# Two-layer trunk on Trainium2: forty residual tiles of the gate weights made on GpSimd instead of VectorE

## Chip, cores and metric

The kernel runs on one core of a Trainium2 chip. The metric is the device time of one execution in microseconds (us); the time of a kernel is the median of its runs. A core has TensorE (PE, matrix products; its weight loads are shown apart as PEld), VectorE (DVE), ScalarE (ACT), GpSimd (POOL) and SyncE (SP, which here issues DMAs). Each engine works through its own queue in order and waits on semaphores for the others.

## The reference

For 256 tokens of width 2048, two layers in float32:

```python
for l in range(DEPTH):
    h = rms_norm(x, pre_mix_norm[l])
    m = hybrid_mixer(h, l, ...)          # in-projection, two kinds of attention, o-projection
    x = x + rms_norm(m, post_mix_norm[l])
    h = rms_norm(x, pre_ffn_norm[l])
    f = (silu(h @ w_gate[l]) * (h @ w_up[l])) @ w_down[l]      # 2048 -> 5632 -> 2048
    x = x + rms_norm(f, post_ffn_norm[l])
```

The case is about `h @ w_gate` and `h @ w_up`.

## The kernel before, in words

**Every weight is used once, in two pieces.** The weights come from memory as tiles of 128 x 2 x 512 float32 (512 KB): one *K pair*, that is 2 x 128 rows of the inner dimension, by 512 columns. They are stored in the order of use (`weights_in_turn`). For each tile SP issues a DMA (L230 into a `raw` buffer of 4, or L219 into a `G` buffer of 3), ACT makes `hi`, the tile rounded to the PE's short float32 format (`float32r`, L351), and VectorE makes the residual `lo = raw - hi` (L354). `hi` and `lo` have six buffers each. The tokens are split the same way into `sh` and `sl`, and a product is three matmuls: sh·hi + sh·lo + sl·hi (`product`, L1116 to L1118).

**Gate and up.** The 5632 columns are cut into 11 chunks of 512. A chunk runs over 8 K pairs (`kp`, in the order 0 to 7; chunk 0 has an order of its own), each with a gate tile and an up tile. It has four sums in PSUM banks, `c11`, `c12`, `c21`, `c22`: two halves of the tokens, each with gate and up. Most K pairs go through `eight`: eight products of 128x128 by 512. Some, in each chunk `SEVEN = (2, 4, 5, 6)`, in chunk 0 (4, 6), in chunk 1 (4, 5, 6), in chunks 7 and 9 (2 to 6), go through `seven`, a scheme of Strassen's kind with seven products. It needs sums of the weights: GpSimd's queue issues an accumulating DMA that adds a part of the gate tile onto the up tile `T` as it loads (L298), VectorE makes two further sums in place, t2 (L334) and G (L335, which overwrites the gate tile), and the sums are split like the weights (ACT L319, VectorE L320, tiles `Th`, `Tl`). The gate tile of such a pair lies in a `G` buffer, and its own `hi` and `lo` must be made before L335 overwrites it. The seven products put four extra sums (p1, p6, p7, q5) into the other four PSUM banks.

**The end of a chunk.** After the last `seven` of a chunk ACT and VectorE fold the four extra sums into four SBUF tiles `w` (`shared_part`, ACT copy L1157, VectorE L1158 to L1161). With that their banks come free, and the next chunk's `c` sums start in them. When the last K pair is done, VectorE adds the `c` banks to `w` (L1308, L1310), ACT makes the silu (L1309), and VectorE multiplies (L1311, two SBUF inputs). A little later PE transposes the result (L1317) and ACT copies it to `act`, the input of the down projection.

**What sets the order.** The program is written in program order, `weights()` makes the tiles four ahead of their use (`LOOKAHEAD`), and a scheduler orders each engine's queue when the program is built. Two hints around the change: `behind()` has the first two `lo` made after a `shared_part` come behind its last sum in VectorE's queue, and `after_rests()` has some other VectorE work come behind the latest `lo`, for which each VectorE `lo` is appended to the list `rests`.

So around a chunk's end VectorE's queue holds, mixed: the last splits of the old chunk, the first splits of the new one (kp 0, 1, 2), the four sums of `shared_part`, and the sums of the `c` banks.

Of the kernel before, what the change touches and what calls it, by code (L numbers as in the profile page):

```python
# [9 lines left out]
F32 = mybir.dt.float32  # L10
# [3 lines left out]
ALU = mybir.AluOpType  # L14
# [10 lines left out]
FF = 5632  # L25
CW = 512
# [22 lines left out]
FORESEEN = {7: (3, 5), 9: (3, 5)}  # L49
AHEAD_AT = 8  # L50
AHEAD_PACE = 2
FORM_AT = {(0, 1): 4, (0, 2): 6, (0, 5): 5, (1, 3): 2, (4, 3): 3}
DOWN_SEVEN = ((4, 7, 10, 12, 15, 17, 20), (3, 5, 8, 10, 13, 15, 18))

# [22 lines left out]
def weight_order():  # L77

    order = []

    def queue_pair(name, l, kp, c):
        order.append((name, l, kp, c))
        return len(order) - 1

    plan = []
    sevens, plain, own = set(), set(), set()
    for l in range(L):
        lay = {"in": {}, "o": {}, "gate": {}, "up": {}, "down": {}}
        for n, (ca, cb) in enumerate(PAIRS):
            for kp in IN_ORDER if n else range(KT // 2):  # L90
                lay["in"][ca, kp] = queue_pair("w_in", l, kp, ca)
                lay["in"][cb, kp] = queue_pair("w_in", l, kp, cb)
                if kp in IN_NOW[n]:
                    plain.add(lay["in"][cb, kp])
        order_o = [(c, kp) for kp in KP_O for c in (0, 1)]
        order_o += [(c, kp) for kp in LATE_O for c in (2, 3)] + [(c, kp) for c in (2, 3) for kp in LAST_O]
        lay["order_o"] = order_o
        for c, kp in order_o:
            lay["o"][c, kp] = queue_pair("w_o", l, kp, c)
            if c == 3 and kp in O_SEVEN:  # L100
                own.add(lay["o"][c, kp])
        for c in range(FF // CW):
            for kp in FIRST_ORDER if c == 0 else range(KT // 2):
                lay["gate"][c, kp] = queue_pair("w_gate", l, kp, c)
                lay["up"][c, kp] = queue_pair("w_up", l, kp, c)
                if kp in gate_sevens(c):
                    sevens.add(lay["up"][c, kp])
        for half in range(2):
            for kp in range(FF // P // 2):
                for c in (2 * half, 2 * half + 1):  # L110
                    lay["down"][c, kp] = queue_pair("w_down", l, kp, c)
                if kp in DOWN_SEVEN[half]:
                    sevens.add(lay["down"][2 * half + 1, kp])
        plan.append(lay)
    return order, plan, sevens, plain, own
# [48 lines left out]
def kernel(  # L164
# [15 lines left out]
    nc = tc.nc  # L180
# [19 lines left out]
    order, plan, sevens, plain, own = weight_order()  # L200
    stream = [weights_in_turn[i].rearrange("p (k n) -> p k n", k=2) for i in range(len(order))]

    ready = {}
    raws, loads = [], []
    fed = [0]

    def fetch(upto):
        while len(raws) < min(upto, len(stream)):
            i = len(raws)
            for j in range(i, min(i + EARLY + 1, mix_raw[3])):  # L210
                if j in sevens and j not in sums and not (j in foreseen and j > i + 1):
                    summed(j)
            if i in sevens:
                raws.append(sums[i])
                continue
            if i + 1 in sevens:
                g = mix_raw[0].tile([P, 2, CW], F32, tag="G", bufs=mix_raw[1], name=f"G{i}")
                with not_ahead(i):
                    loads.append(nc.sync.dma_start(g, stream[i]))  # L219
                raws.append(g)  # L220
                continue
            if i in own or i + 1 in own:
                raw = mix_pool[0].tile([P, 2, CW], F32, tag="v", bufs=2, name=f"V{i}")
            elif i in plain or i + 1 in plain:
                raw = late_room([P, 2, CW], f"GU{i}")
            else:
                raw = wpool.tile([P, 2, CW], F32, tag="raw", bufs=4, name=f"raw{i}")
            mixing = bool({i, i + 1} & (own | plain))
            with not_ahead(i) if mixing else nullcontext():
                loads.append(nc.sync.dma_start(raw, stream[i]))  # L230
            raws.append(raw)
            if not mixing:
                usual.append((i, loads[-1]))
# [10 lines left out]
    def foresee(l):  # L244
# [4 lines left out]
        def summed_up(i):  # L249
            g, u = tiles[i]  # L250
            k = kept.tile([P, 4, CW], F32, name=f"foreseen{i}")
            with after_rests():
                sums_in_place(g, u, True)
            nc.gpsimd.dma_start(k[:, 0:2, :], u)
            nc.gpsimd.dma_start(k[:, 2:4, :], g)
            foreseen[i] = k

        for n, i in enumerate(jobs):
            tiles[i] = [x_pool[0].tile([P, 2, CW], F32, tag="W", bufs=2 * len(jobs), name=f"{q}{i}") for q in ("Gf", "Tf")]
            for t, j in zip(tiles[i], (i - 1, i)):  # L260
                with in_turn():
                    nc.sync.dma_start(t, stream[j])
                yield AHEAD_PACE
            if n:
                summed_up(jobs[n - 1])
            yield AHEAD_PACE
        yield AHEAD_PACE
        summed_up(jobs[-1])
# [72 lines left out]
    def feed(upto):  # L341
        fetch(upto)
        while fed[0] < min(upto, len(stream)):
            i = fed[0]
            raw = raws[i]
            if i in sevens or i in plain or i in own:
                ready[i] = mixed_weights(i)
                fed[0] += 1
                continue
            hi = wpool.tile([P, 2, CW], F32R, tag="hi", bufs=6, name=f"hi{i}")  # L350
            nc.scalar.activation(hi, raw, AF.Copy)  # L351
            lo = wpool.tile([P, 2, CW], F32R, tag="lo", bufs=6, name=f"lo{i}")
            with behind():
                rest = nc.vector.tensor_tensor(out=lo, in0=raw, in1=hi.bitcast(F32), op=ALU.subtract)  # L354
            ready[i] = (hi, lo)
            fed[0] += 1
            rests.append(rest)
# [4 lines left out]
    def behind():  # L362

        if held[1] == 0:
            return nullcontext()
        held[1] -= 1
        return tc.issue_after(held[0].ins)

    def after_rests():

        return tc.issue_after(rests[-1].ins)
# [5 lines left out]
    def weights(i, ahead):  # L377
        feed(i + 1 + ahead)
        return ready[i]
# [20 lines left out]
    def put_away(nm, n):  # L400

        if n == 0:
            away.append(kept.tile([P, NT, D], F32, name=f"away_{nm}"))
        t, h = divmod(n, 2)
        with in_turn():
            nc.sync.dma_start(away[-1][:, t, h * D // 2 : (h + 1) * D // 2], xs[t][h])
# [760 lines left out]
    for l in range(L):  # L1167
# [17 lines left out]
        for n, (c, kp) in enumerate(plan[l]["order_o"][:16]):  # L1185
# [5 lines left out]
            if n in (9, 11):  # L1191
                kp = O_SEVEN[(n - 9) // 2]
# [4 lines left out]
        for kp in LATE_O:  # L1197
            i, j = (plan[l]["o"][c, kp] for c in (2, 3))
# [6 lines left out]
            hi, lo = weights(i, LOOKAHEAD)  # L1205
# [13 lines left out]
        with tc.manual_schedule(engines={mybir.EngineType.Activation, mybir.EngineType.DVE}):  # L1219
            feed(idx + 6)  # L1220
            for n, (c, kp) in enumerate(last_o):
                unit({0: accs[c, 0]}, mix, idx + n, kp, (0,), False, kp == LAST_O[-1], 0)
                if kp == LAST_O[-1]:
                    evac_sum(pool, accs[c, 0], mg, ssm, gpost, c, 0, f"o{l}")
            rescale(mg, ssm, 0, f"o{l}")
            for n, (c, kp) in enumerate(last_o):
                feed(idx + 7 + n)
                fetch(min(idx + 12 + n, idx + 12))
                unit({1: accs[c, 1]}, mix, idx + n, kp, (1,), False, kp == LAST_O[-1], 0)
                transposed(0, 32 + l * KT, xT, cols=(n,))  # L1230
                if (c, kp) == (2, LAST_O[-1]):
                    evac_sum(pool, accs[2, 1], mg, ssm, gpost, 2, 1, f"o{l}", True)
# [17 lines left out]
        def pair_sums(kp):  # L1250
            f = pool.tile([P, 2, S], F32, tag="t2", name=f"f{l}_{kp}")
            for kk in range(2):
                st = xT[2 * kp + kk]
                nc.vector.tensor_tensor(out=f[:, kk, :], in0=st[:, 0, :].bitcast(F32), in1=st[:, 1, :].bitcast(F32), op=ALU.add)
            forms[kp] = token_sums(pool, gu if kp in SEVEN else None, len(SEVEN), f[:, 0, 0:P], f[:, 1, 0:P], f[:, 0, P:S], f[:, 1, P:S], f"{l}_{kp}")
# [18 lines left out]
        for c in range(FF // CW):  # L1274
# [9 lines left out]
            for n, kp in enumerate(order):  # L1284
                if n == 1 and c in AWAY_AT:
                    put_away(f"ffn{l}", AWAY_AT.index(c))
                if (c, n) in FORM_AT:
                    with after_rests():
                        pair_sums(FORM_AT[c, n])
                if kp not in mine:  # L1290
# [41 lines left out]
        for half in range(2):  # L1332
# [74 lines left out]
            for t in range(NT):  # L1407
# [4 lines left out]
                for c in cc:  # L1412
                    for kp in range(nkp - tail, nkp):
# [3 lines left out]
                        hi, lo = weights(plan[l]["down"][c, kp], LOOKAHEAD)  # L1417
# [66 lines left out]
```

## Time and profile before

| | us |
|---|---|
| median of 3 runs | 2190.61 (2189.62 to 2191.96) |
| the profiled execution: its span | 2189.2 |
| PE busy | 2174.7 (99%) |
| VectorE busy | 1921.7 (88%) |
| ACT busy | 1378.0 (63%) |
| GpSimd busy | 144.2 (7%) |
| SP's DMA queue, share of 16 engines' span | 58.9% |

The profile is of one further execution; it lists a span, from the first to the last instruction, and no other time of its own, so the span is what sums are made against. It stands 1.4 us under the median of the runs. The engines' busy times don't add up to the span, since they work beside each other. In a timeline a row is: start, duration, engine, line, operation, out<-in, shape, how many rows of the same kind were taken together, and in brackets the idle time before it and what ended it. Instructions of one engine overlap a little: the next one of VectorE starts about 0.08 us before the last one ends, so a 1.22 us instruction takes 1.14 us of the queue; a PE matmul of 0.39 us takes 0.23.

### The profile page before, as it was taken

The page shows a single profiled execution, that of the slowest core. Times are in us where ns is not written, and L with a number is a line of the kernel's source. Part 1 is how long each engine was busy: PE and PEld are TensorE (multiplying, and loading weights), DVE is VectorE, ACT ScalarE, POOL GpSimd, SP SyncE. Part 2 cuts the span into 40 slices and gives each one's busy share as a digit, 9 for nine tenths or more (in the row PEclk, how much of TensorE's full clock was granted, in tenths as well). Part 3 has the DMA queues.
Part 4 walks back from the last instruction along what each step waited for, and adds up shares of the span by engine and source line. Part 5 has one row for each costly group of instructions (what it writes and reads, how often), then busy time and mean ns, then how long its engine had stood idle before and what let it go on. Part 6 is the DMA issues. An engine that isn't in the chain of part 4 may idle for free.

```text
span 2189.2 us, 28686 instructions
## 1 busy us (share of the span) xinstructions
PE 2174.7 (99%) x9980; PEld 1787.4 (82%) x9980; DVE 1921.7 (88%) x2647; ACT 1378.0 (63%) x2063; POOL 144.2 (7%) x199
## 2 busy tenths in 40 slices
PE   9999999999999999999999999999999999999998
PEld 7888888788888888888878888887788888888886
DVE  7888659999999999989878886699999999999997
ACT  7666665756656666666665656657566566666664
POOL 1100000010010000000010000000000100000000
PEclk9999999999999999999999999999999999999999
DMA  9545577587687786767465555775866877867673
GB/s 322 194 164 173 192 243 267 184 274 234 206 282 235 229 273 210 245 210 257 146 240 173 183 173 183 256 258 195 269 214 226 274 241 232 263 213 234 207 264 101
DMA packets 146033, 489.30 MB, mean 224 GB/s; under 512 B 16592, under 2 KB 17616, under 8 KB 145376
## 3 DMA queue, kind: packets, MB, share of 16 engines
q1 hardware_dynamic: 127712, 450.72, 58.9%
q0 software_dynamic: 17600, 36.22, 8.3%
q8 instruction: 78, 1.28, 0.2%
q10 hardware_dynamic: 576, 0.54, 0.1%
q14 instruction: 67, 0.55, 0.1%
HBM read 470.63 MB, written 16.78 MB: 223 GB/s over the span
## 4 chain that ended last, share of the span: by engine, by line
PE 92%; DVE 5%; ACT 1%; issue 1%; DMA 1%; DVEq 0%; ACTq 0%
PE c L1117 9%; PE c L1118 9%; PE c L1116 9%; PE in L1116 7%; PE in L1118 7%; PE in L1117 7%; PE dn L1368 4%; PE dn L1366 4%; PE dn L1365 4%; PE p L1117 2%; PE p L1118 2%; PE p L1116 2%; PE o L601 2%; PE o L603 2%; PE o L602 2%; DVE lo L354 1%
## 5 line engine op out<-in xcount | busy, mean ns | idle before, releaser
L354 DVE TENSOR_TENSOR lo<-raw,hi 128x1024 fp32r<-128x1024 f32 x514 | 615.2, 1219 | 90.7 <-ACT hi L351 89.8
L351 ACT ACTIVATE hi<-raw 128x1024 fp32r<-128x1024 f32 x514 | 531.3, 1055 | 183.1 <-DMA raw<-in_weights_in_turn_dram 51.3
L1116 PE MATMUL c<-hi,xF 128*128 128x512 f32 x806 | 317.2, 394 | 0.1
L1117 PE MATMUL c<-lo,xF 128*128 128x512 f32 x806 | 314.4, 390 | 1.2 <-DVE lo L354 1.0
L1118 PE MATMUL c<-hi,xF 128*128 128x512 f32 x806 | 314.0, 390 | 0.0
L1117 PEld LDWEIGHTS c<-lo,xF 128*128 128x128 f32 x806 | 151.5, 188 | 33.2 <-DVE lo L354 3.3
L1118 PEld LDWEIGHTS c<-hi,xF 128*128 128x128 f32 x806 | 151.3, 188 | 32.0 <-DVE xF L525 0.4
L1116 PEld LDWEIGHTS c<-hi,xF 128*128 128x128 f32 x806 | 151.4, 188 | 30.3 <-ACT xF L520 0.5
L298 POOL DMA_DIRECT2D T<-in_weights_in_turn_dram x106 | 92.2, 869 | 1257.8 <-DMA T<-in_weights_in_turn_dram 434.6
L1365 PE MATMUL dn<-hi,jh 128*128 128x512 f32 x432 | 168.2, 389 | 0.0
L1366 PE MATMUL dn<-lo,jh 128*128 128x512 f32 x432 | 168.1, 389 | 0.0
L354 DVE TENSOR_TENSOR lo<-G,hi 128x1024 fp32r<-128x1024 f32 x114 | 138.8, 1218 | 21.1 <-ACT hi L351 21.0
L319 ACT ACTIVATE hi<-T 128x1024 fp32r<-128x1024 f32 x114 | 119.7, 1050 | 41.9 <-PE c L1118 23.9
L320 DVE TENSOR_TENSOR lo<-T,hi 128x1024 fp32r<-128x1024 f32 x114 | 138.8, 1217 | 3.2 <-ACT hi L319 2.3
L351 ACT ACTIVATE hi<-G 128x1024 fp32r<-128x1024 f32 x114 | 120.0, 1053 | 30.1 <-PE c L1118 17.4
L319 ACT ACTIVATE Th<-G 128x1024 fp32r<-128x1024 f32 x106 | 111.8, 1055 | 36.8 <-DVE G L335 35.3
L320 DVE TENSOR_TENSOR Tl<-G,Th 128x1024 fp32r<-128x1024 f32 x106 | 129.1, 1218 | 5.5 <-ACT Th L319 5.3
L1368 PE MATMUL dn<-hi,jl 128*128 128x512 f32 x432 | 133.0, 390 | 0.0
L1116 PE MATMUL in<-hi,xT 128*128 128x512 f32 x328 | 131.0, 401 | 1.1 <-ACT hi L921 1.1
L1116 PE MATMUL in<-hi,xI 128*128 128x512 f32 x328 | 131.2, 401 | 0.0
L335 DVE TENSOR_TENSOR G<-G,T 128x1024 f32<-128x1024 f32 x106 | 129.3, 1220 | 1.7
L1117 PE MATMUL in<-lo,xI 128*128 128x512 f32 x328 | 128.1, 390 | 0.3 <-DVE lo L354 0.3
(485 smaller groups left out, 4786.7 us busy)
## 6 DMA issues: line engine op xcount, KB each, us to landing
raw<-in_weights_in_turn_dram SPq DMA_DIRECT2D x514, 512.0 KB, 4.7
G<-in_weights_in_turn_dram SPq DMA_DIRECT2D x114, 512.0 KB, 5.8
T<-in_weights_in_turn_dram SPq DMA_DIRECT2D x106, 512.0 KB, 6.4
T<-in_weights_in_turn_dram POOLq DMA_DIRECT2D x106, 256.0 KB, 7.2
GU<-in_weights_in_turn_dram SPq DMA_DIRECT2D x32, 512.0 KB, 6.5
Gf<-in_weights_in_turn_dram SPq DMA_DIRECT2D x8, 512.0 KB, 6.0
Tf<-in_weights_in_turn_dram SPq DMA_DIRECT2D x8, 512.0 KB, 6.7
V<-in_weights_in_turn_dram SPq DMA_DIRECT2D x8, 512.0 KB, 5.2
```

The source lines that it names most:

```text
L298: nc.gpsimd.dma_start(sums[i][:, 0, :], stream[i - 1][:, 0, :], accum_op=ALU.add)
L319: nc.scalar.activation(h, w, AF.Copy)
L320: nc.vector.tensor_tensor(out=l, in0=w, in1=h.bitcast(F32), op=ALU.subtract)
L335: nc.vector.tensor_tensor(out=g, in0=g, in1=t2.unsqueeze(1).to_broadcast([P, 2, CW]), op=ALU.add)
L351: nc.scalar.activation(hi, raw, AF.Copy)
L354: rest = nc.vector.tensor_tensor(out=lo, in0=raw, in1=hi.bitcast(F32), op=ALU.subtract)
L1116: nc.tensor.matmul(a, sh, hi, start=first, stop=False, skip_group_check=open_sums[0])
L1117: nc.tensor.matmul(a, sh, lo, start=False, stop=False, skip_group_check=open_sums[0])
L1118: nc.tensor.matmul(a, sl, hi, start=False, stop=last, skip_group_check=open_sums[0])
L1365: nc.tensor.matmul(accs[c, t], sh, hi[:, kk, :], start=first, stop=False, skip_group_check=open_sums[0])
L1366: nc.tensor.matmul(accs[c, t], sh, lo[:, kk, :], start=False, stop=False, skip_group_check=open_sums[0])
L1368: nc.tensor.matmul(accs[c, t], sl, hi[:, kk, :], start=False, stop=last, skip_group_check=open_sums[0])
```

## The change

For the gate tiles of the second and third K pair (kp 1 and 2) in chunks 1 to 10 of both layers, 2 x 10 x 2 = 40 tiles, GpSimd computes `lo = raw - hi`, the same subtraction, in place of VectorE. All other residuals stay on VectorE. Of the 40 tiles 22 are plain (`raw`: kp 1 everywhere, and kp 2 in chunk 1) and 18 are gate tiles of a `seven` (`G`: kp 2 in chunks 2 to 10). A helped tile isn't appended to `rests`, and `behind()` doesn't count it. The buffers and DMAs are the same.

```diff
@@ -49,6 +49,7 @@
+HELPED = (1, 2)
...
@@ -200,6 +201,8 @@
+    helped = {lay["gate"][c, kp] for lay in plan for c in range(1, FF // CW) for kp in HELPED}
+
...
@@ -350,6 +353,11 @@
             hi = wpool.tile([P, 2, CW], F32R, tag="hi", bufs=6, name=f"hi{i}")
             nc.scalar.activation(hi, raw, AF.Copy)
             lo = wpool.tile([P, 2, CW], F32R, tag="lo", bufs=6, name=f"lo{i}")
+            if i in helped:
+                nc.gpsimd.tensor_tensor(out=lo, in0=raw, in1=hi.bitcast(F32), op=ALU.subtract)
+                ready[i] = (hi, lo)
+                fed[0] += 1
+                continue
             with behind():
                 rest = nc.vector.tensor_tensor(out=lo, in0=raw, in1=hi.bitcast(F32), op=ALU.subtract)
             ready[i] = (hi, lo)
```

## The prediction, as it was put on record

> **What bounds the kernel now.** First the head of the page, then gate/up cut into windows (columns: window, its length, busy time and count of PE, PEld, DVE, ACT and POOL, clock, DMA share, GB/s). In layer 0 chunk 1 runs from about 441 to 484.3 us and chunks 2 to 10 from there to 858.1; the third window is layer 1's chunk 1.
>
> ```profile
> span 2189.2 us, 28686 instructions
> ...
> PE 2174.7 (99%) x9980; PEld 1787.4 (82%) x9980; DVE 1921.7 (88%) x2647; ACT 1378.0 (63%) x2063; POOL 144.2 (7%) x199
> ```
> ```profile
> 441.00:484.30 43.30, 42.66 (x190) 34.47 (x189) 41.41 (x56) 25.03 (x29) 4.37 (x5) 1.00 0.80 257
> 484.30:858.10 373.80, 373.67 (x1683) 308.98 (x1682) 352.71 (x386) 233.11 (x270) 27.82 (x32) 1.00 0.73 236
> 1530.00:1573.00 43.00, 41.98 (x186) 33.57 (x185) 40.41 (x54) 24.52 (x29) 3.82 (x5) 1.00 0.79 253
> ```
>
> PE is the bound. Over nine chunks it stands still for 373.80 - 373.67 = 0.13 us, so nothing done for VectorE can win anything there. Only the two chunks 1 hold something: 0.64 and 1.02 us. VectorE is nearly full beside it: 352.71 of 373.80, 39.2 a chunk of 41.5. Its waits in chunks 3 to 10 (us in total, times, longest) say where it has room:
>
> ```profile
> DVE lo L354 <- ACT hi L351: 9.5, 6, 1.8
> DVE w L1158 <- PE p L1118: 6.4, 7, 1.6
> ```
>
> It waits for inputs that ACT and PE have not made, so in these chunks it is ahead of need.
>
> **The price of one piece on GpSimd.** Forty tiles (kp 1 and 2, ten chunks, two layers) leave VectorE; the built program has 2557 VectorE instructions for 2597 and 244 for 204 on GpSimd, all else counted alike. No 128x1024 subtraction on GpSimd is in this trace. Its small ones are, with VectorE rows of the same moments:
>
> ```profile
> 48.60 0.46 POOL L874 TENSOR_TENSOR ra<-tok,rope_sb 128x128 f32<-128x128 f32 x1 [12.19 <-DMA lams<-in_lambda_k_dram]
> 49.02 0.32 POOL L875 TENSOR_TENSOR rb<-tok,rope_sb 128x64 f32<-128x64 f32 x1
> ...
> 52.91 1.54 POOL L874 TENSOR_TENSOR ra<-tok,rope_sb 128x128 f32<-128x128 f32 x1
> ...
> 96.04 0.33 POOL L875 TENSOR_TENSOR rb<-tok,rope_sb 128x64 f32<-128x64 f32 x1
> ```
> ```profile
> 52.90 1.23 DVE L354 TENSOR_TENSOR lo<-GU,hi 128x1024 fp32r<-128x1024 f32 x1 [1.50 <-ACT hi L351]
> 54.04 0.95 DVE L324 TENSOR_TENSOR GU<-GU,GU 128x512 f32<-128x512 f32 x1
> ...
> 95.98 1.37 DVE L1000 TENSOR_TENSOR w<-in,w 128x512 f32<-128x512 f32 x2 [0.46 <-PE in L1118]
> ```
>
> Sixty-four elements more cost 0.14 us: 2.2 ns an element, 0.18 + 1024 x 2.2 = 2.4 us for a tile. That is an estimate over a factor of eight; 2.1 to 2.55 covers a row's rounding. VectorE takes 1.14 a tile, start to start. **The two exclude each other.** GpSimd's 0.46 job begun at 52.91 lasted 1.54: it ended at 54.45, 0.32 after VectorE's two-operand subtraction ended at 54.13. The next one of VectorE's, 128x512, then took 0.95, against 0.68 for that shape below. So beside VectorE's SBUF-SBUF work a GpSimd piece starts when VectorE's instruction ends and then holds VectorE off for about 2.28 us (2.4 less what overlaps). Sums that read PSUM are spared: two of them at 95.98 took 1.37, or 0.69 each, with a GpSimd piece running. A tile moved therefore costs VectorE between -1.14 (all beside PSUM sums or idle time) and 2.28 - 1.14 = +1.14.
>
> The Trainium skill, page "SBUF — State Buffer", section "SBUF: two separate sides", says the same of a lock between a GpSimd operation and a VectorE one with two SBUF inputs, and page "Perfetto Trace Analysis", section "Optimizing Scalar/DVE Operations", warns that offloading between these two might not help because of it. By that rule alone the change is the second rival below; the rows agree on the lock, and show that it spares PSUM sums.
>
> **Chunks 3 to 10.** One chunk's end, 6 to 7, by timelines of ACT, VectorE and PE; the last VectorE row is mid-chunk, 20 us earlier:
>
> ```profile
> 685.53 1.06 ACT L351 ACTIVATE hi<-raw 128x1024 fp32r<-128x1024 f32 x1
> ...
> 693.86 1.05 ACT L351 ACTIVATE hi<-G 128x1024 fp32r<-128x1024 f32 x1
> ```
> ```profile
> 684.60 1.22 DVE L320 TENSOR_TENSOR Tl<-G,Th 128x1024 fp32r<-128x1024 f32 x1
> ...
> 687.59 0.69 DVE L1158 TENSOR_TENSOR w<-p,w 128x512 f32<-128x512 f32 x1 [0.64 <-PE p L1118]
> ...
> 689.65 0.68 DVE L1161 TENSOR_TENSOR w<-q,w 128x512 f32<-128x512 f32 x1
> 690.24 2.35 DVE L354 TENSOR_TENSOR lo<-raw,hi 128x1024 fp32r<-128x1024 f32 x2
> 692.51 0.68 DVE L1308 TENSOR_TENSOR w<-c,w 128x512 f32<-128x512 f32 x1
> ...
> 695.57 1.21 DVE L354 TENSOR_TENSOR lo<-G,hi 128x1024 fp32r<-128x1024 f32 x1
> 696.70 0.74 DVE L1311 SCALAR_TENSOR_TENSOR w<-w,rs_ffn,w 128x512 f32<-128x512 f32 x1
> ```
> ```profile
> 686.18 0.39 PE L1117 MATMUL p<-Tl,sh 128*128 128x512 f32 x1
> ...
> 691.85 0.39 PE L1118 MATMUL c<-hi,xF 128*128 128x512 f32 x1
> ```
> ```profile
> 664.84 1.23 DVE L354 TENSOR_TENSOR lo<-G,hi 128x1024 fp32r<-128x1024 f32 x1 [1.73 <-ACT hi L351]
> ```
>
> Second pair: its hi ends at 685.53 + 1.06 = 686.59. GpSimd waits for the VectorE piece then running and holds from about 686.96 to 689.24, beside idle time and the PSUM sums of L1158 to L1161: nothing is delayed. VectorE has one piece fewer at 690.24, but its next sum reads a bank that PE completes only at 691.85 + 0.39 = 692.24, so that gain ends as waiting.
>
> Third pair: hi ends at 694.91; VectorE is in a PSUM sum, GpSimd holds about 695.05 to 697.33. VectorE no longer makes the piece of 695.57, wants L1311 (two SBUF inputs) then, and gets it at 697.33: it ends near 698.0 for 697.44 before, **0.55 us late**. Mid-chunk VectorE stood idle 1.73 us (0.9 to 1.8 across the first row of its waits), which swallows the lag. In chunks 7 and 9 it must pass to the tightest place, a Tl that is ready at 684.60 + 1.22 = 685.82 for a PE start of 686.18: 0.36 of room here, against 0.55 at most; the 0.19 that could be left over, in two chunks of each layer, stays in the range. I take **0**.
>
> New waits: VectorE's in-place sum G (L335) now waits for GpSimd, which reads that G; by program order it stands behind both L1311 and the up tile's piece, so GpSimd's end at 697.33 comes first. Some raw loads of SP wait for GpSimd in place of VectorE, about as early. In GpSimd's queue the accumulating T loads (L298) stand behind pieces that wait for their hi; behind a late T wait ACT's hi, then PE. With four tiles of look-ahead I cost these at nothing.
>
> **Chunk 0 to 1, and chunk 1.** Here the second pair's hi ends amid VectorE's pieces:
>
> ```profile
> 435.60 1.06 ACT L351 ACTIVATE hi<-raw 128x1024 fp32r<-128x1024 f32 x1 [1.18 <-DMA raw<-in_weights_in_turn_dram]
> ```
> ```profile
> 436.12 2.35 DVE L354 TENSOR_TENSOR lo<-raw,hi 128x1024 fp32r<-128x1024 f32 x2
> ...
> 440.98 0.68 DVE L1161 TENSOR_TENSOR w<-q,w 128x512 f32<-128x512 f32 x1
> ```
> ```profile
> 443.06 0.39 PE L1116 MATMUL c<-hi,xF 128*128 128x512 f32 x1
> ...
> 472.35 0.39 PE L1118 MATMUL c<-hi,sl 128*128 128x512 f32 x1
> 473.23 0.50 PE L1117 MATMUL p<-Tl,sh 128*128 128x512 f32 x1 [0.50 <-DVE Tl L320]
> 473.57 0.40 PE L1118 MATMUL p<-Th,sl 128*128 128x512 f32 x1
> ```
>
> GpSimd gets in between the two pieces of 436.12, holds to about 439.6, and all behind moves by 2.28: L1161 ends at 441.66 + 2.28 = 443.94, and PE's product of 443.06 goes into the bank it empties: **+0.9 us** a layer. Later in the chunk VectorE has 1.14 us less to do per tile, and PE's present waits should go. At 473.23 the trace lists 0.50, but from 472.35 start to start PE lost 0.88 - 0.23 = 0.65, and the next start came 0.11 late: 0.76 for 0.50, a factor of 1.5 for listed waits. So 0.64 x 1.5 = 1.0 in layer 0 and 1.02 x 1.5 = 1.5 in layer 1: **-2.5**.
>
> **Chunk 1 to 2.** The same collision, late in a chunk with little room; the waits are VectorE's from 484.3 to 520.5:
>
> ```profile
> 477.11 2.35 DVE L354 TENSOR_TENSOR lo<-raw,hi 128x1024 fp32r<-128x1024 f32 x2
> ...
> 517.37 1.22 DVE L320 TENSOR_TENSOR Tl<-G,Th 128x1024 fp32r<-128x1024 f32 x1
> ```
> ```profile
> 518.64 0.50 PE L1117 MATMUL p<-Tl,sh 128*128 128x512 f32 x1
> ```
> ```profile
> DVE w L1158 <- PE p L1118: 0.5, 1, 0.5
> DVE lo L354 <- ACT hi L351: 0.4, 2, 0.2
> DVE w L1311 <- ACT w L1309: 0.3, 1, 0.3
> ```
>
> 2.28 - 1.14 = 1.1 late from the second pair and 0.55 from the third; idle time takes back up to 1.2, leaving 0.45 at a Tl ready at 518.59 for a start at 518.64: **+0.4** a layer. If none is taken back, 1.6.
>
> **Sum.** 2 x 0.9 - 2.5 + 2 x 0.4 = **+0.1 us**. The profiled execution's span is 1.4 below the median of 2190.61; the difference is put on the median: **2190.7**. With no gap taken back and holds at the long end: + 2.4 + 1.6, near 2194.5; if the collisions cost nothing, below 2190.61 by what is in the next case.
>
> **Rivals.**
> 1. All waits of the chunks 1 go and nothing is added: 2190.61 - 2.5, less the 0.26 of chunks 2 to 10 in two layers, **2187.8**. For it: -1.14 a tile on a 39.2-us engine. Against: the collision at 436.66. Chance 0.08, of which 0.02 for more than 0.2%, should waits outside gate/up shrink too.
> 2. **The lock turns VectorE into the bound** (slower): each hold falls beside SBUF-SBUF work, +2.28 net per chunk. 39.2 + 2.28 = 41.5 against 41.5; it decides as soon as any wait can't be worked through. Of the 0.8 us a chunk that L1158 waits for PE I take half: 0.4 x 9 x 2 = 7, with chunks 1 at +1.1 or so a layer, **2200**. Against: the second pair's place beside PSUM sums in the steady chunks. Chance 0.12.
> 3. **A GpSimd piece is far longer than the small rows say** (slower). For it, from the groups of GpSimd lines:
>
> ```profile
> L450 POOL TENSOR_SCALAR_AFFINE_SELECT negones<-negones 128x128 f32<-128x128 f32 x1 | 3.0, 2953 | 5.8 <-DVE negone L449 5.8
> ```
>
> That is another operation. From a hold of 4.4 us the third pair's lag, 0.55 + 2.1, exceeds 1.73 + 0.36 and PE waits in every chunk; at 4.5, 0.7 x 9 + 2.2 x 3 a layer, **2216**. Chance 0.08.
>
> **Chances.** Forecast 0.72, its own range 2187.5 to 2194.5; rivals 0.08, 0.12, 0.08. 0.2%, 4.4 us, is about what a measurement of this kernel can tell from no change: faster 0.02, same 0.78, slower 0.20. The range leaves out the third rival and a little more: 2187 to 2200.
>
> **What would show it.** GpSimd's subtractions near 2.4 us each; L354 on raw and G with 40 fewer; in steady chunks VectorE's idle time up by nearly 1.14 a chunk and PE still at 0.13 over nine; a new PE wait near 443 for L1161; the wait at 473.23 gone. It is wrong if PE waits for lo or Tl in the steady chunks, if PSUM sums stretch beside GpSimd, or if a T lands late.

## The result, and the profile after

The changed kernel takes 2193.42 us (median of 20 runs, 2191.22 to 2194.57), the kernel before in as many runs 2189.93 (2189.21 to 2191.96). The ratio is 1.0014, with a 95% interval of 1.0007 to 1.002: some 3 us slower. The interval leaves 1 out, so the loss is clear of the noise, but it lies inside the 0.2% that was called no change. The profiled execution lost 2.8 us:

```profile
span 2192.0 us, 28747 instructions
...
PE 2174.8 (99%) x9980; PEld 1787.4 (82%) x9980; DVE 1912.2 (87%) x2607; ACT 1374.1 (63%) x2063; POOL 254.7 (12%) x239
```

PE's busy time is unchanged (2174.7 before), so the 2.8 us are PE waiting. The same windows as before, for layer 0's chunk 1, its chunks 2 to 10, and layer 1's chunks 2 to 10 (they end up to 3 us further right and are up to 2.2 us longer, since the two kernels are shifted against each other):

```profile
441.00:485.00 44.00, 43.87 (x198) 35.98 (x197) 42.06 (x56) 27.25 (x33) 11.90 (x9) 1.00 0.83 273
485.00:861.00 376.00, 373.96 (x1682) 308.79 (x1681) 350.37 (x367) 229.57 (x270) 71.88 (x48) 1.00 0.73 234
...
1575.00:1953.00 378.00, 376.51 (x1692) 310.57 (x1691) 348.80 (x370) 232.03 (x272) 71.12 (x48) 1.00 0.73 235
```

Chunk 1 now has 0.13 us without PE, for 0.64. But chunks 2 to 10, which had 0.13 in each layer, have 2.04 and 1.49. The question is which of the nine. Each chunk leaves a mark in PE's timeline: the transposes of its result (L1317 before, L1325 after), some 6 us into the next chunk. The marks of chunks 6 and 7, first before, then after:

```profile
702.28 0.38 PE L1317 MATMUL actT_ps<-ident,w 128*128 128x128 f32 x2
...
743.37 0.39 PE L1317 MATMUL actT_ps<-ident,w 128*128 128x128 f32 x2
```
```profile
701.06 0.38 PE L1325 MATMUL actT_ps<-ident,w 128*128 128x128 f32 x2
...
743.40 0.27 PE L1325 MATMUL actT_ps<-ident,w 128*128 128x128 f32 x1
```

The changed kernel is 1.2 us ahead at the first mark and level at the second: chunk 7 cost it 1.26. Done for all marks, this gives the table on which the rest stands: what each stretch cost (+) or won (-) against the kernel before, in us. The experiments, but for e6 and e8, are in it already, by their labels. "To 1" is all that lies ahead of the mark of chunk 1: in layer 0 from the start of the program, in layer 1 from the mark of layer 0's chunk 10. These stretches vary by some 0.5 between executions (e2, whose edit lies outside them, shows -0.02 and +0.53), the others by 0.1. Each row is one execution.

| | to 1 | 2-6 | 7 | 8 | 9 | 10 | layer 1: to 1 | 2-6 | 7 | 8 | 9 | 10 |
|---|---|---|---|---|---|---|---|---|---|---|---|---|
| changed kernel | -1.08 | -0.15 | +1.26 | +0.01 | +1.22 | +0.01 | -0.85 | -0.10 | +1.72 | +0.51 | 0.00 | 0.00 |
| e1_order | -1.33 | -0.08 | +0.53 | +0.04 | +0.64 | +0.04 | -0.93 | -0.07 | +0.67 | 0.00 | +0.73 | 0.00 |
| e2_before_swap | -0.02 | 0.00 | +0.90 | +0.04 | +2.16 | +0.04 | +0.53 | +0.07 | +2.23 | 0.00 | +0.80 | 0.00 |
| e3_second_pair | -1.42 | -0.10 | -0.04 | +0.04 | +0.17 | +0.04 | -1.35 | -0.01 | +0.13 | +0.08 | +0.34 | +0.04 |
| e4_third_pair | +0.22 | -0.09 | +0.53 | +0.04 | +0.56 | +0.04 | -0.13 | -0.11 | +0.27 | 0.00 | 0.00 | +0.03 |
| e5_queues | -0.60 | -0.11 | 0.00 | 0.00 | 0.00 | 0.00 | -0.99 | -0.07 | -0.04 | +0.04 | -0.04 | +0.04 |
| e7_vector | -0.15 | -0.10 | -0.04 | +0.04 | +0.04 | +0.04 | +0.21 | -0.03 | +0.30 | +0.11 | -0.04 | +0.04 |
| e9_second_pinned | -0.98 | -0.11 | 0.00 | 0.00 | +1.21 | 0.00 | -1.56 | -0.06 | +0.04 | +0.08 | 0.00 | 0.00 |
| e10_from_two | -1.08 | -0.13 | 0.00 | 0.00 | 0.00 | 0.00 | -1.24 | -0.08 | -0.04 | +0.04 | -0.04 | +0.04 |

The changed kernel wins 1.9 us by the chunks 1 and loses 4.7 in chunks 7 and 9 and the chunk behind one of them. These are the chunks with five Strassen-like pairs, two of which (kp 3 and 5) have sums made earlier and kept in memory. A kept pair's T tile comes in by loads of SP's queue, one part from the kept sums (`T<-foreseen`) and one from the weights.

**Where chunk 7 loses.** PE at the end of the changed kernel's chunk 7; VectorE in its middle and at its end; ACT in its middle; and last, ACT in the kernel before:

```profile
725.82 0.39 PE L1124 MATMUL p<-Th,sh 128*128 128x512 f32 x1
727.17 0.50 PE L1125 MATMUL p<-Tl,sh 128*128 128x512 f32 x1 [0.96 <-DVE Tl L323]
```
```profile
709.27 1.23 DVE L362 TENSOR_TENSOR lo<-G,hi 128x1024 fp32r<-128x1024 f32 x1 [1.46 <-ACT hi L354]
...
713.26 1.22 DVE L323 TENSOR_TENSOR lo<-T,hi 128x1024 fp32r<-128x1024 f32 x1 [0.91 <-ACT hi L322]
...
725.89 1.23 DVE L323 TENSOR_TENSOR Tl<-G,Th 128x1024 fp32r<-128x1024 f32 x1
```
```profile
708.18 1.06 ACT L354 ACTIVATE hi<-G 128x1024 fp32r<-128x1024 f32 x1 [1.85 <-DMA G<-in_weights_in_turn_dram]
712.17 1.06 ACT L322 ACTIVATE hi<-T 128x1024 fp32r<-128x1024 f32 x1 [2.93 <-DMA T<-in_weights_in_turn_dram]
```
```profile
710.29 1.06 ACT L319 ACTIVATE hi<-T 128x1024 fp32r<-128x1024 f32 x1 [1.66 <-PE c L1118]
```

PE waits for a Tl that VectorE makes late. VectorE is late because it stood idle 1.46 and 0.91 us some 15 us earlier, for ACT, and has worked without a gap since; ACT stood idle 1.85 and 2.93 us for two transfers. In the kernel before ACT made the second of these hi's at 710.29, and what it waited for was PE. So the chain begins at the DMAs. SP's queue there, before and after:

```profile
702.59 0.33 SPq L219 DMA_DIRECT2D G<-in_weights_in_turn_dram  x1
703.73 0.33 SPq L288 DMA_DIRECT2D T<-foreseen  x1
704.11 0.42 SPq L289 DMA_DIRECT2D T<-in_weights_in_turn_dram  x1
704.86 0.33 SPq L219 DMA_DIRECT2D G<-in_weights_in_turn_dram  x1
```
```profile
702.17 1.46 SPq L222 DMA_DIRECT2D G<-in_weights_in_turn_dram  x2
704.44 0.33 SPq L291 DMA_DIRECT2D T<-foreseen  x1
704.82 1.62 SPq L292 DMA_DIRECT2D T<-in_weights_in_turn_dram  x1
```

Before: G of kp 5, T of kp 5, G of kp 6. After: both G's (the x2), then T. ACT needs this T before the second G, but T goes out behind it and shares the DMA engines with a G that could have waited. No line of the diff touches these loads; the scheduler orders each queue anew for the changed program. In the same places VectorE's and ACT's queues are also changed: the split of the T of kp 3 stands behind another split of that kept pair (`Tl<-second`) and behind the last split of kp 2.

### The profile page after: what moved, and what is told of

Same layout as the page of the kernel before. It is cut to its first block, busy times and chain, and to the rows that moved or that the text cites. A ratio compares the mean times of both kernels' runs of the same rounds, so it can differ in the third digit from the quotient of the medians.

```text
span 2192.0 us, 28747 instructions
## 1 busy us (share of the span) xinstructions
PE 2174.8 (99%) x9980; PEld 1787.4 (82%) x9980; DVE 1912.2 (87%) x2607; ACT 1374.1 (63%) x2063; POOL 254.7 (12%) x239
## 4 chain that ended last, share of the span: by engine, by line
PE 84%; DVE 8%; issue 3%; DMA 3%; ACT 1%; POOL 0%; SPq 0%; DVEq 0%; ACTq 0%; POOLq 0%
PE c L1125 7%; PE c L1126 7%; PE c L1124 7%; PE in L1124 7%; PE in L1126 7%; PE in L1125 7%; PE dn L1376 4%; PE dn L1373 4%; PE dn L1374 4%; PE o L609 2%; PE o L611 2%; PE o L610 2%; DVE lo L362 2%; DMA T<-in_weights_in_turn_dram 2%; DVE Tl L323 2%
## 5 line engine op out<-in xcount | busy, mean ns | idle before, releaser
L362 DVE TENSOR_TENSOR lo<-raw,hi 128x1024 fp32r<-128x1024 f32 x492 | 593.1, 1223 | 90.2 <-ACT hi L354 89.5
L322 ACT ACTIVATE Th<-T 128x512 fp32r<-128x512 f32 x106 | 66.7, 629 | 153.6 <-DVE T L337 144.5
L323 DVE TENSOR_TENSOR lo<-T,hi 128x1024 fp32r<-128x1024 f32 x114 | 144.9, 1271 | 8.9 <-ACT hi L322 8.3
L362 DVE TENSOR_TENSOR lo<-G,hi 128x1024 fp32r<-128x1024 f32 x96 | 117.4, 1223 | 19.7 <-ACT hi L354 19.4
```

The lines of the kernel that those rows point to most:

```text
L322: nc.scalar.activation(h, w, AF.Copy)
L323: nc.vector.tensor_tensor(out=l, in0=w, in1=h.bitcast(F32), op=ALU.subtract)
```

## The experiments

Theory Q: the loss comes from the new order of the queues in chunks 7 and 9; the first expectations take it as SP's order alone. Theory L, its rival: it comes from GpSimd's hold on VectorE in the chunks with the least room. The labels are the table's.

**e1_order: SP's order put back.**

```diff
-                with not_ahead(i):
+                with tc.issue_after(early[i - 1].ins) if i - 1 in early else not_ahead(i):
                     loads.append(nc.sync.dma_start(g, stream[i]))
...
                 loads.append(nc.sync.dma_start(two[0][:, 1, :], stream[i][:, 1, :]))
+                early[i] = loads[-1]
```

> The changed kernel with all 40 pieces on GpSimd, and four loads of SP's queue moved back: in chunks 7 and 9 of both layers the G tile of K pair 6 is issued behind the three T loads of K pair 5 (those kept in memory), as in the kernel before, instead of ahead of them. Nothing else in any queue moves. Theory Q (the loss comes from SP's order: T lands about 3.3 us late, and ACT, VectorE and PE wait for it): the transposes of chunks 7, 8 and 9 lose nothing against those of the kernel before, so the 1.26 + 1.22 us of layer 0 and 1.72 + 0.51 of layer 1 go: the span of 2192.0 falls by 4.7 to about 2187.3, 0.1% under the kernel before. Theory L (the loss comes from GpSimd holding VectorE off in chunks that have no slack): the span stays at 2192, and PE waits for Tl at the end of chunks 7 and 9 as before.

Measured: span 2189.7, median 2191.44 (before, in the same runs, 2190.36; ratio 1.0006, 0.9997 to 1.0015). The loss of chunks 7 to 9 falls from 4.7 to 2.6 us: 0.53, 0.64, 0.67, 0.73. Neither theory's number: SP's order is worth 2.1 us of the loss, and something else the rest. Theory Q as it stood here, SP's order alone, is too small. ACT's hi of T still waits for its load, but less; SP's issue of it, and VectorE just before that:

```profile
711.26 1.06 ACT L323 ACTIVATE hi<-T 128x1024 fp32r<-128x1024 f32 x1 [2.23 <-DMA T<-in_weights_in_turn_dram]
```
```profile
704.25 0.33 SPq L291 DMA_DIRECT2D T<-foreseen  x1
```
```profile
703.00 1.22 DVE L324 TENSOR_TENSOR lo<-T,hi 128x1024 fp32r<-128x1024 f32 x1
```

T is issued at 704.25, though this kernel is 1.4 us ahead of the kernel before, which issued it at 703.73: 1.9 late. It goes out right behind VectorE's split of the T of kp 3, which ends at 704.22 and frees a buffer; in the kernel before that split ends at 703.71.

**e2_before_swap: the kernel before with SP's new order.** The two G's are fetched ahead of the T of kp 5 (the edit in part):

```diff
+                    if j in foreseen and j - 4 in foreseen:
+                        for k in (j - 1, j + 1):
+                            g_first[k] = mix_raw[0].tile([P, 2, CW], F32, tag="G", bufs=mix_raw[1], name=f"G{k}")
+                            with not_ahead(i):
+                                loads.append(nc.sync.dma_start(g_first[k], stream[k]))
                     summed(j)
...
```

> The kernel before, no piece on GpSimd, with the same four G loads of SP's queue put ahead of the T loads of K pair 5, as the changed kernel has them. Theory Q: T lands 2 to 3.5 us late in chunks 7 and 9, VectorE then waits for ACT and PE for Tl; 1 to 2 us in each of the four chunks, a span of 2193 to 2197 for 2189.2. Theory L: no change, 2189.2.

Measured: span 2195.9, median 2195.54 for 2190.36, ratio 1.0024 (1.0014 to 1.0034). 0.9, 2.2, 2.2 and 0.8 us in the four chunks, nothing between them, with no piece on GpSimd at all. (The profiled execution is the longest of its runs, 2.1 us above their median, so the typical loss is rather 5 us than this one's 6.7.) ACT and PE in chunk 7:

```profile
712.99 1.06 ACT L334 ACTIVATE hi<-T 128x1024 fp32r<-128x1024 f32 x1 [4.19 <-DMA T<-in_weights_in_turn_dram]
```
```profile
727.99 0.50 PE L1132 MATMUL p<-Tl,sh 128*128 128x512 f32 x1 [0.61 <-DVE Tl L335]
```

The same picture as in the changed kernel: theory Q, and it is enough by itself. ACT's and VectorE's queues have the order of the kernel before here. In SP's queue the second G goes out at 704.85, as in the kernel before (704.86); T, now behind it, goes out at 705.23 and not at 703.73.

**e3_second_pair and e4_third_pair: one K pair alone** (`HELPED = (1,)`, `HELPED = (2,)`).

> The change for the second K pair alone (kp 1, 20 raw tiles). By itself the schedule then leaves the T loads of K pair 5 ahead of that G load. Theory Q: no loss in chunks 7 to 9, the gain of chunk 1 stays (1.1 us in layer 0, 0.85 in layer 1): 2187 to 2187.5. Theory L: the piece that starts at the end of chunks 7 and 9 (3.8 us each in the changed kernel) costs about half of the loss: 2189 to 2190.

> The change for the third K pair alone (kp 2, 18 G tiles and 2 raw). The schedule again puts the G load of K pair 6 ahead of the T loads of K pair 5 in chunks 7 and 9. Theory Q: the whole loss of about 4.7 us stays, less what chunk 1 wins: 2191 to 2193. Theory L: about half of it: 2189 to 2190.5.

Measured: e3 span 2187.1, median 2190.11 for 2190.36 (1.0, 0.999 to 1.0009), where the profiled execution is 1.3 us under the median; e4 span 2190.5, median 2192.63 (1.0012, 1.0002 to 1.0021). The queue order is bad only where the third pair is moved; with the second alone chunks 7 and 9 lose 0.6 in all. But e4 loses 1.4 us there, not the 4.7 that theory Q gave, and 0 in layer 1's chunk 9; its span lies at the upper end of theory L's range. So two things go with the third pair, and e4 doesn't tell them apart: VectorE's order in it is another one again. The pair also shows whose the win of the chunks 1 is: e3 has 1.42 and 1.35 up to their marks, e4 loses 0.22 and wins 0.13. It is the second pair's.

**e5_queues: all queues of chunks 7 and 9 as before, all 40 pieces on GpSimd.** Beside e1's edit, ACT's and VectorE's last splits of kp 2 are put off until T of kp 3 is split, and those of the kept pair go behind them:

```diff
-        split(hi, lo, u)
+        done = split(hi, lo, u)
+        if i - 2 in put_off:
+            done = split(*put_off.pop(i - 2), done)
...
-        split(th[:, 0:2, :], tl[:, 0:2, :], g)
+        if i + 2 in foreseen and i - 2 not in foreseen:
+            put_off[i] = th[:, 0:2, :], tl[:, 0:2, :], g
+        else:
+            split(th[:, 0:2, :], tl[:, 0:2, :], g)
```

> The changed kernel, all 40 pieces on GpSimd, with the queues of chunks 7 and 9 put back as the kernel before has them: on VectorE and ACT the splits of T of K pair 3 go ahead of the last splits of K pair 2 and of the two kept tiles again, and SP issues T of K pair 5 ahead of the G of K pair 6. Beside the kernel of e1_order it differs in these few places alone. Theory Q (the rest of the loss, 0.53 + 0.64 us in layer 0 and 0.67 + 0.73 in layer 1, comes from VectorE's changed order: it frees a buffer of T and one of G about 1.9 and 0.8 us later, so their loads go out later): it goes, and the span falls from 2189.7 to about 2187.1. Theory L (the rest is GpSimd's hold of 2.3 us on VectorE at L1311): it stays, 2189.7.

Measured: span 2187.8, median 2189.05 for 2190.47 (0.9993, 0.9984 to 1.0002). Chunks 7 to 9 cost 0.00 in layer 0 and 0.04 at most in layer 1. ACT's hi of T of kp 5 in chunk 7, and VectorE at the piece that stands ahead of it:

```profile
709.88 1.07 ACT L326 ACTIVATE hi<-T 128x1024 fp32r<-128x1024 f32 x1 [1.95 <-DMA T<-in_weights_in_turn_dram]
```
```profile
695.00 2.15 DVE L1329 SCALAR_TENSOR_TENSOR w<-w,rs_ffn,w 128x512 f32<-128x512 f32 x1
```

With 0.7 us of lead that is 0.3 later than the 710.29 of before, where the changed kernel was 3.1 later. The pieces made for chunks 7 and 9 are where they were and hold VectorE as long, 2.15 for this instruction as in the changed kernel (below). Theory L falls for these chunks; the whole 4.7 us was queue order. Put back one after the other, SP's order gave 2.1 us and VectorE's and ACT's, which set when a buffer comes free, 2.6. The two don't simply add up: in e2 SP's order alone cost 5 to 6 us.

**e6_double: each piece made twice** (`for _ in range(2):` around the GpSimd subtraction, on e5_queues).

> The kernel of e5_queues with every piece made twice by GpSimd (the same subtraction into the same tile), so that each holds twice as long. By the sum of the prediction, lag 0.55 + 2.28 = 2.8 us on VectorE against 1.73 + 0.36 of room, PE waits 0.7 us or so in every chunk from 3 on, and more in chunks 1, 7 and 9: a span of 2197 to 2215. If VectorE gets its turn between the two, or the room is larger than thought: below 2192.

Measured: span 2236.2, median 2236.63 (1.0207, 1.0191 to 1.0222): 47 us, about 2 a chunk. GpSimd's third-pair pieces and VectorE in chunk 2:

```profile
490.48 2.40 POOL L368 TENSOR_TENSOR lo<-G,hi 128x1024 fp32r<-128x1024 f32 x1 [1.75 <-ACT hi L364]
...
493.43 2.69 POOL L368 TENSOR_TENSOR lo<-G,hi 128x1024 fp32r<-128x1024 f32 x1
```
```profile
491.25 2.17 DVE L1330 SCALAR_TENSOR_TENSOR w<-w,rs_ffn,w 128x512 f32<-128x512 f32 x1
493.35 3.86 DVE L328 TENSOR_TENSOR lo<-T,hi 128x1024 fp32r<-128x1024 f32 x1
```

VectorE gets its turn between the two, and is blocked by both: 2.17 for 0.74, then 3.86 for 1.22. The sum had the right kind of end, PE waiting in every chunk, and was too small: it let only the third pair's hold grow, while the second pair's outlasts the PSUM sums beside it too (at 704.07, the end of chunk 6, VectorE's subtraction after them takes 3.51 for 1.22). So the steady chunks have room for one hold of this length, not for two. Not all of the 47 us is waiting: PE's busy time is 2193.0 us for 2174.7, with a granted clock of 0.97 from 445 to 500 us and 0.99 from 500 to 880, where the kernel before has 1.00. Why the clock is lower isn't shown.

**e7_vector: VectorE makes the pieces, the hints as in the change** (`nc.vector` for `nc.gpsimd` in the new branch).

> The changed kernel with the 40 pieces made by VectorE, but not counted in the two hints for the order (rests and behind), as in the changed kernel. If what chunk 1 wins (0.95 us in layer 0, 0.85 in layer 1) comes from the order of the queues, it is there too, 2187 to 2188.5. If it comes from VectorE's shorter work, chunk 1 is as before, 2189 or more.

Measured: span 2189.6, median 2191.27 for 2190.47 (1.0005, 0.9996 to 1.0014). Chunks 1 win nothing (-0.15 and +0.21, within what these stretches vary). So the win of the chunks 1 is not the hints': it comes with the pieces' leaving VectorE.

**e8_last_pair: the last K pair in place of the second and third** (`HELPED = (7,)`).

> The 20 pieces of the last K pair (kp 7, raw) in place of those of kp 1 and 2. Their hi is made while VectorE runs its subtractions of two SBUF operands back to back, some 8 us long. If GpSimd gets the port at the end of one such instruction (the prediction's reading), each piece holds VectorE 2.3 us, 1.14 more than it saves, and PE waits 0.3 to 0.8 us a chunk: 2194 to 2204. If VectorE's back-to-back run keeps GpSimd out, VectorE isn't delayed, the piece lasts up to 8 us, and PE waits for its lo: the GpSimd rows of L357 take 5 us or more, and the span is above 2195.

Measured: span 2212.3, median 2212.8 (1.0103, 1.0084 to 1.0121), 23.1 us for 20 pieces. GpSimd and VectorE in chunk 2:

```profile
513.75 2.90 POOL L357 TENSOR_TENSOR lo<-raw,hi 128x1024 fp32r<-128x1024 f32 x1 [13.86 <-ACT hi L354]
```
```profile
513.18 1.22 DVE L323 TENSOR_TENSOR lo<-T,hi 128x1024 fp32r<-128x1024 f32 x1
514.43 2.77 DVE L337 TENSOR_TENSOR T<-T 128x512 f32<-128x512 f32 x1
```

GpSimd gets in when the running instruction ends (514.40) and ends its piece at 516.65; VectorE's next, 0.68 by itself, takes 2.77. Most chunks pay about 1.0 a piece (1.02 in chunks 8 and 10), chunks 7 and 9 nothing, layer 0's chunk 1 3.3 and its chunk 4 2.2. Both readings gave the direction; the first had the mechanism, with 0.3 to 0.8 a chunk too small a price.

**e9_second_pinned: the second pair, both T loads ahead of both G's** (e5's edits, and the G of kp 5 behind the T of kp 6; the expectation calls it the G of K pair 4).

> GpSimd makes the second K pair alone (20 raw tiles), and SP's queue in chunks 7 and 9 is set so that T of K pairs 6 and 5 goes ahead of the G of K pairs 4 and 6. In e3_second_pair a G load went ahead of T of K pair 6, which landed late in chunk 9 and cost 0.17 to 0.34 us there. If order of loads is all that is left in these chunks, those go and the span is 0.5 us under that of e3_second_pair, 2186.6; if G of K pair 4 is now late, VectorE waits for its hi and the span is 2187 or above.

Measured: span 2187.8, median 2189.41 for 2190.47 (0.9996, 0.9987 to 1.0005). A miss: layer 1's chunk 9 no longer loses, but layer 0's loses 1.21. There the other arm of the expectation holds: ACT waits 3.63 us for this G and makes its hi at 792.87, where the kernel before, though 1.1 us behind, made it at 790.39. Three neighbouring loads, and each order of them has its own price.

**e10_from_two: e5_queues without the two third-pair pieces of chunk 1** (`if (c, kp) != (1, 2)`, 38 pieces).

> The kernel of e5_queues without the two raw tiles of the third K pair of chunk 1, which VectorE makes again (38 pieces on GpSimd). If their hold beside VectorE's first work of chunk 1 costs part of what that chunk wins, chunk 1 wins 1.0 us in layer 0 and 1.4 in layer 1, as in e3_second_pair, in place of 0.9 and 1.07: a span of 2187.4. If not, VectorE's extra 1.14 us makes it lose: 2188 or more.

Measured: span 2186.6, median 2188.31 for 2190.47, ratio 0.999 (0.9981 to 0.9999): faster than both kernels, than the kernel before by 2.2 us. Its chunks 2 to 10 in the two layers:

```profile
484.00:858.00 374.00, 373.87 (x1684) 309.32 (x1683) 350.30 (x367) 231.08 (x270) 69.58 (x48) 1.00 0.73 234
...
1571.00:1948.00 377.00, 376.88 (x1698) 311.74 (x1697) 352.67 (x372) 234.15 (x273) 69.58 (x49) 1.00 0.73 236
```

PE stands still for 0.13 and 0.12 us, as before the change. The sum was near, but the place isn't shown: chunks 0 and 1 together win 1.08 and 1.24 where e5 had 0.60 and 0.99, and that difference is about what these stretches vary from one execution to the next. From chunk 0's mark to chunk 1's layer 0 even wins less than in e5, 0.45 for 0.90, and layer 1 about the same, 1.19 for 1.07.

## Why the prediction was right, and where not

The forecast, no change beyond 0.2%, held, and 2193.4 lies in its own range. But 2190.7 came from terms that are off in both directions, and that is in part luck: the range reached to 2194.5 for collisions that cost nothing, and the 4.7 us that brought the time there stand in no term.

- **The price of a piece: right.** Estimated 2.4 us. The shortest of the 22 pieces from `raw` takes 2404 ns and of the 18 from `G` 2393 (median 2405). The means are longer, since waits for VectorE are in them:

```profile
L357 POOL TENSOR_TENSOR lo<-raw,hi 128x1024 fp32r<-128x1024 f32 x22 | 67.8, 3080 | 357.6 <-ACT hi L354 357.6
L357 POOL TENSOR_TENSOR lo<-G,hi 128x1024 fp32r<-128x1024 f32 x18 | 45.5, 2525 | 29.0 <-issue 19.2 <-ACT hi L354 9.8
```

- **The steady chunks: right, with their mechanism.** At the end of chunk 6, GpSimd, then VectorE's second L1311 (now L1319):

```profile
685.50 2.50 POOL L357 TENSOR_TENSOR lo<-raw,hi 128x1024 fp32r<-128x1024 f32 x1 [21.51 <-ACT hi L354]
...
693.67 2.40 POOL L357 TENSOR_TENSOR lo<-G,hi 128x1024 fp32r<-128x1024 f32 x1 [4.84 <-issue]
```
```profile
694.47 2.15 DVE L1319 SCALAR_TENSOR_TENSOR w<-w,rs_ffn,w 128x512 f32<-128x512 f32 x1
```

  The second pair lies beside PSUM sums and delays nothing; the third blocks L1319, which ends at 696.62. With 1.2 us of lead that is 0.4 later than the 697.44 of before; 0.55 was forecast. Chunks 2 to 6 pay nothing. VectorE's idle time in chunks 2 to 10 grew, by the windows above, only from 21.1 to 25.6 us, 0.5 a chunk, and not by nearly 1.14: the time for which it is blocked counts as busy (2.15 for 0.74 above).
- **Chunks 7 and 9: the failed step.** It said "I take **0**", by VectorE's lag alone, and put the new waits and SP's loads "at nothing" with the look-ahead as cover. What was compared of the built program was how many instructions each queue has, not their order. The third pair's move turned the order of SP's, ACT's and VectorE's queues there, and that costs 4.7 us (e1, e2, e5). The hold itself costs 0 there. The prediction had named two signs of this itself, a T that lands late and PE waiting for Tl; both came in these chunks.
- **Chunk 0 to 1, +0.9 a layer: wrong.** GpSimd and VectorE at that place:

```profile
436.63 3.99 POOL L357 TENSOR_TENSOR lo<-raw,hi 128x1024 fp32r<-128x1024 f32 x1 [22.58 <-ACT hi L354]
```
```profile
435.97 2.37 DVE L362 TENSOR_TENSOR lo<-raw,hi 128x1024 fp32r<-128x1024 f32 x2
...
439.05 0.69 DVE L1167 TENSOR_TENSOR w<-p,w 128x512 f32<-128x512 f32 x1
...
440.85 0.68 DVE L1169 TENSOR_TENSOR w<-q,w 128x512 f32<-128x512 f32 x1
```

  GpSimd did not get between VectorE's two pieces: these took 2.37 as ever. It waited until 438.34, held 2.28 beside PSUM sums, and the last sum ended at 441.53, not at 443.94. Four more pieces of layer 0 (at 476.20, 602.16, 726.71 and 810.78) and four of layer 1 were passed over in the same way, where e8's twenty were not. What decides it stays open.
- **Chunks 1, -2.5: too large.** With all that lies ahead of them in the table they won 1.08 and 0.85, from chunk 0's mark to their own 0.95 and 0.85. In layer 1 a new wait takes the place of the old one:

```profile
1567.30 0.50 PE L1125 MATMUL p<-Tl,sh 128*128 128x512 f32 x1 [0.59 <-DVE Tl L323]
```

- **Chunk 2, +0.4 a layer:** nothing there; -0.15 and -0.10 up to chunk 6. The collision it came from is one of those where GpSimd was passed over.

So the sum of -2.5, +1.8, +0.8 and 0 was, as measured, -1.9 for the first two together, -0.25 up to chunk 6, and +4.7. The Trainium skill, page "SBUF — State Buffer", section "SBUF: two separate sides", has the lock held for a whole instruction and the other engine fully blocked. The traces agree where the two meet (2.15 for 0.74 at L1319, 2.77 for 0.68 in e8), and a sum with one operand in PSUM runs through it (0.69 at 439.05 and around, with GpSimd at work).

The second rival, VectorE as the bound, is what e8 shows: there a piece lies beside SBUF-SBUF work and costs on average 23.1 / 20 = 1.15 us, as the upper end of its price, 1.14, said. That the two agree so closely is chance, since the chunks pay from 0 to 3.3. The first rival's 2187.8 is a median, 2.8 us under the kernel before; with the queues put back the change comes part of the way, to medians 1.4 us under it (e5, 2189.05) and 2.2 under it (e10, 2188.31).

## What to carry to other kernels

When a scheduler orders the queues, compare the order of every queue before and after, DMA queues first, and not only the counts: an edit on one engine can reorder loads ten microseconds away, and here that was more than all the direct effects together. The experiments fixed it by naming, in the program, the instruction behind which a load is issued. In these runs a piece moved to GpSimd was free where VectorE read PSUM or waited, and blocked VectorE, for up to its whole length, where it read two SBUF operands, except where GpSimd was passed over; look at what VectorE does when the piece's input arrives. And tables of a mark per stage, one row for each kernel, find a loss of 0.5 us that the total can't show.

## What the runs showed of the hardware

- VectorE blocked by GpSimd shows as one long instruction, not as idle time: 2.15 for 0.74, 3.86 for 1.22.
- Of two loads in one queue the order alone moved a consumer by 2 to 3 us: ACT's hi of T began at 712.99 in e2, for 710.29, with the same four loads between 702 and 707 us. Of these 2.7 us, 1.5 passed before T went out, behind a G that itself went out no earlier than before.
